# Summing two tokens' accumulators over partitions: sixteen one-column products become eight streaming products in four column groups; one bank for a pair of transposes; weight sums issued earlier

## The chip, the core and the metric

The kernel is one program on one core of a Trainium2 chip. The metric is the device time of one execution in microseconds (us); lower is better. The engines are named as in the profile: PE (TensorE matmul), PEld (its weight load), DVE (VectorE), ACT (ScalarE), POOL (GpSimd) and SP (SyncE, which here issues DMAs).

## The reference

One layer of a streaming encoder, batch 1, 1024 tokens and 16 learned meta tokens ahead of them, 1024 features:

```python
u = rmsnorm(h, norm_mix_g)
z = u @ w_in                        # q, k, v, o gates of 4 mLSTM and 4 retention heads
mixed = concat(mlstm heads, retention heads) * gates     # 2048 features
h = h + mixed @ w_out               # the mixer's output product
a = causal_dwconv(u2 @ w_up); h = h + (silu(a) * (u2 @ w_gate)) @ w_down   # u2 = rmsnorm(h)
out = rmsnorm(h, norm_final_g)[:, N_META:]
```

## The kernel before, in words

Activations lie transposed, with features on the 128 partitions and tokens in the columns; `resid` holds the residual as 8 feature blocks (KB = 8) by tokens. A matmul with full accuracy is done as three: both operands are split into a high and a low part in a rounded type, and hi*hi, lo*hi and hi*lo are added in PSUM (lines 378 to 380, 388 to 390, 554 to 556).

The program has these stages, with their times in the trace:

- **The heads**, up to about 700 us. `ORDER` is the list of heads, [4,0,1,2,3,5,6,7]; below, the place in this list is i. For each head, the o gates of this head are merged with its scan, and the v product of the next head is merged with `post_steps` of this one (norm of a head, two transposes, multiplication by the gate). `post_steps(h, p)` for the token third p returns the statistics and `half(0)`, `half(1)`. Each half takes a PSUM tile of the tag `tr`, which has one bank; transposes into it; and has DVE multiply out of it (line 908). After that, `tables(nxt)` loads the next retention head's decay table A (line 529), masks it on DVE (line 533) and scales it on ACT (line 536).
- **The output product** `mixed @ w_out`, about 700 to 863 us, by the object `mixw` in a scheme of seven products in place of eight, in steps called "1", "65", "73", "4" and "2". Its outputs are added to `resid` by DVE (lines 698 and 713). Two of the scheme's operands, called 65 and 73, are sums of blocks of w_out. They are made ahead of time in DRAM by `wsum` (lines 188 to 197): two DMAs of 512 KB on SP (line 194), then five adding DMAs on POOL (line 196), each of which waits for the one before on the same sum. There are 8 such sums "w" for w_out and 11 sums "d" for w_down. `wsum_next()` pops the next one. In the heads it is called after one of the o groups of each i from 1 to 7, and once in a v group, for i = 4.
- **The last two tokens** don't fit this scheme (columns T-2 and T-1 of `resid`). `last_two(k)` (line 178 on) loads block k of w_out and has DVE multiply it by the two tokens' values, one value per partition, and add it to the accumulator `acc` (128 partitions by 2 tokens by 1024 outputs, line 181). In the end `acc` must be summed over its partitions and added to `resid`. This is done in step "4" by lines 1186 to 1190: 16 matmuls, each with a 128x128 piece of `acc` as the stationary operand and a column of ones as the moving one, and one DVE addition of the 16 resulting columns.
- **The norm of the second half of the tokens** (514 columns, the last two among them), then the feed-forward products `pup` and `pga` from about 863 us. ACT squares each block of `resid` (line 1095), DVE adds the squares (line 1099), PE sums over partitions (`pcb`, lines 298 and 309) and spreads the result (`prb`, line 309), ACT copies it (line 313), DVE scales `resid` (line 1109), and ACT and DVE make the hi and lo operands `xh` and `xl` (lines 1037 and 1038). The quarters of the first half follow in the same manner and give `uh_g` and `ul_g`.

The order within each engine is not the order of the source: a scheduler places each instruction on its engine by estimated times, so that an edit moves its neighbours too. Pools of buffers are named by tags; `ftile` is one of five slots.

Of the kernel before, what the change touches and what calls it, by code (L numbers as in the profile page):

```python
# [17 lines left out]
P = 128  # L18
# [45 lines left out]
def body(ctx, tc, h_in, vecs, cst, mask_in, rot, w_v0, w_v, w_fm, w_out, w_up, w_gate, w_down, out):  # L64
# [133 lines left out]
    def wsum_next():  # L198
        if wsums:
            wsum(*wsums.pop(0))  # L200
# [157 lines left out]
    def v_group(h, c, tag="pp"):  # L358
        t0, L = CH[c]
        nv = 264 if h == HF else 256  # L360
        U = [need(("v", h, i), 2 - i) for i in range(2)]
        pv = pp(f"pv{h}_{c}", tag)
        if c == 0:

            for i in range(2):
                for j in range(4):
                    nc.tensor.matmul(pv[32 * j:32 * j + 32, :nv], ug[:, 4 * i + j, :], U[i][2][:, j * nv:(j + 1) * nv],
                                     start=i == 0, stop=i == 1, tile_position=(0, 32 * j))
            t = wk.tile([P, WMAX], F32, tag="cv", name=f"v0_{h}", bufs=2)[:META]
            nc.scalar.copy(t[:, :nv], pv[:META, :nv])  # L370
            for j in range(1, 4):
                nc.vector.tensor_tensor(t[:, :nv], pv[32 * j:32 * j + META, :nv], t[:, :nv], ALU.add)
            return lambda: v_evac(h, 0, META, t)
        for kb in range(KB):
            hi, lo, _ = U[kb // 4]
            o = (kb % 4) * nv
            a, b = uh[kb][:, t0:t0 + L], ul[kb][:, t0:t0 + L]
            nc.tensor.matmul(pv[:L, :nv], a, hi[:, o:o + nv], start=kb == 0, stop=False)  # L378
            nc.tensor.matmul(pv[:L, :nv], a, lo[:, o:o + nv], start=False, stop=False)  # L379
            nc.tensor.matmul(pv[:L, :nv], b, hi[:, o:o + nv], start=False, stop=kb == KB - 1)  # L380
        return lambda: v_evac(h, c, L, pv)
# [40 lines left out]
    def o_group(h, b, p):  # L422
        t0, t1, _ = PIECES[p]
        t0 = max(t0, KEEP)
        n = t1 - t0
        U = need(("o", h, b), 2)
        pt = pp(f"po{h}_{b}_{p}")
        fm_mms(pt, U, t0, t1)
        s = sig(b, p)
        nc.vector.tensor_tensor(s, pt[:, :n], Rb[:, t0:t1], ALU.mult)  # L430
        nc.scalar.activation(s, s, AF.Sigmoid if h < H else AF.Silu)
# [440 lines left out]
    def post_steps(h, p):  # L872
        t0, t1, chs = PIECES[p]
        n = len(chs)
        m = {}

        def stats():
            num, mv, base = outs.pop(p)
            z = mxp.tile([P, 4], F32, tag="z", name=f"z{h}_{p}", bufs=2)
            if h < H:  # L880
                den = base[:, 0:n, DV]
                e2 = cols[:, 2].rearrange("p (c h) -> p h c", h=H)[:, h, chs[0]:chs[0] + n]
                nc.vector.tensor_tensor(z[:, :n], den, den, ALU.mult)
                nc.vector.tensor_tensor(z[:, :n], z[:, :n], e2, ALU.max)
                nc.vector.scalar_tensor_tensor(z[:, :n], z[:, :n], EPS, mv[:, 0:n, 1], ALU.mult, ALU.add)
            else:
                nc.vector.tensor_tensor(z[:, :n], mv[:, 0:n, 1], Re[:, h - H, chs[0]:chs[0] + n], ALU.add)
            nc.scalar.activation(z[:, :n], z[:, :n], AF.Sqrt)
            nc.vector.reciprocal(z[:, :n], z[:, :n])
            nc.vector.scalar_tensor_tensor(mv[:, 0:n, 1], mv[:, 0:n, 0], -1.0, z[:, :n], ALU.mult, ALU.mult)  # L890
            for i, c in enumerate(chs):
                L = CH[c][1]
                nc.scalar.activation(num[i][:L, :DV], num[i][:L, :DV], AF.Identity, bias=mv[:L, i, 1:2], scale=z[:L, i:i + 1])
            m["num"] = num

        def half(b):
            num = m["num"]
            tr = ps.tile([P, 512], F32, tag="tr", name=f"tr{h}_{p}_{b}")
            for i, c in enumerate(chs):
                c0, L = CH[c]  # L900
                nc.tensor.transpose(tr[:, c0 - t0:c0 - t0 + L], num[i][:L, b * P:(b + 1) * P], ident[:L, :L])
            a0 = max(t0, KEEP)
            w = t1 - a0
            g = (V_MLG if h < H else V_RTG) + (h % H) * 2 + b
            i = 2 * h + b

            def mix_into(dst, x0, x1):
                nc.vector.scalar_tensor_tensor(dst, tr[:, x0 - t0:x1 - t0], vec[:, g:g + 1], sig(b, p)[:, x0 - a0:x1 - a0], ALU.mult, ALU.mult)
            if h == 7:
                for q, o in (("A2", MA), ("B2", MB)):  # L910
                    x0, x1 = max(a0, o), min(t1, o + HB)
                    if x0 < x1:
                        mix_into(wact(q, 6 + b)[:, x0 - o:x1 - o], x0, x1)
                if t1 > MB + HB:
                    mix_into(mm[:, i], MB + HB, t1)
                return
            mx = sig(b, p)
            mix_into(mx[:, :w], a0, t1)
            e = min(t1, MB + HB)
            nc.sync.dma_start(mxd[i][:, a0 - MA:e - MA], mx[:, :e - a0])  # L920
            if e < t1:
                nc.vector.tensor_copy(mm[:, i], mx[:, e - a0:w])
        return [stats, lambda: half(0), lambda: half(1)]
# [8 lines left out]
    def merge(main, side, start=0, stop=None):  # L932
        stop = len(main) if stop is None else stop
        done = 0
        for i, m in enumerate(main):
            m()
            if i + 1 > start:
                want = len(side) * min(i + 1 - start, stop - start) // (stop - start)
                while done < want:
                    side[done]()  # L940
                    done += 1
        while done < len(side):
            side[done]()
            done += 1
# [58 lines left out]
    for i, h in enumerate(ORDER):  # L1003
        A = lambda c, h=h: (lambda: scan_a(h, c))
        B = lambda c, h=h: ab(h, c)
        merge([lambda b=b, p=p: (o_group(h, b, p), p == 1 and b and i and wsum_next()) for b in range(2) for p in range(3)],
              [A(0)] + [B(c) for c in range(4 if h < 7 else NCH)])
        if h == 7:
            break
        side = post_steps(h, 0) + [B(4), B(5), B(6)] + post_steps(h, 1) + [B(7), B(8)] + post_steps(h, 2)  # L1010
        nxt = ORDER[i + 1]
        merge([lambda c=c: (v_group(nxt, c)(), c == 4 and i == 4 and wsum_next()) for c in range(NCH)], side)
        if i:
            tables(nxt)
        for kind in "qk":
            for p in range(3):
                qk_group(nxt, kind, p)
# [141 lines left out]
    for t, (st, k) in enumerate(mixw.steps):  # L1159
        if st == "2":  # L1160
            break
        if t == 0:
            mixw.pump()
        if st == "65" and k == 1:
            x = fp.tile([P, 4 * XW], F32, name="wm", tag="xh2", bufs=1)
            last_two(14, x[:, :D])
            last_two(15, x[:, D:2 * D])
        if st == "1" and k:
            mixw.tsum(1, k - 1)
        elif st == "65":  # L1170
            if k == 0:
                mixw.tsum(1, KW - 1)
            if k >= 2:
                mixw.tsum(3, k - 2)
        elif st == "73" and k < 2:
            mixw.tsum(3, KW - 2 + k)
        if t == KW - 1:
            mixw.mms(t)
        for u in range(t, min(t + (3 if st == "4" or (st, k) == ("73", KW - 1) else 2), 4 * KW)):
            mixw.prep(u)  # L1180
            if mixw.steps[u][0] == "73" and u % 2 and u + 7 not in mixw.four:
                mixw.pre4(u + 7)
        if t != KW - 1:
            mixw.mms(t)
        if st == "4" and k == 0:
            pe = pp("pe2", "tr")
            for mb in range(KB):
                for i in range(2):
                    nc.tensor.matmul(pe[:, 2 * mb + i:2 * mb + i + 1], acc[:, i, mb * P:(mb + 1) * P], cs[:, C_M01 + P - 1:C_M01 + P], start=True, stop=True)
            V.tensor_tensor(resid[:, :, T - 2:], pe[:, :2 * KB].rearrange("p (m i) -> p m i", i=2), resid[:, :, T - 2:], ALU.add)  # L1190
        if st == "4":
            some(3)
        if k == KW - 1:
            mixw.give(st)
            if st == "73":
                for b in (2, 6):
                    blocks[b] = fblock(b)
                side += norm_tasks(*BQ[0]) + scale_tasks(*BQ[0], "tr")
# [404 lines left out]
```

## Time and profile before

| | us |
|---|---|
| median of 3 runs | 1546.13 (1542.49 to 1546.73) |
| the profiled execution | 1549.12 |
| its span in the profile | 1547.3 |
| PE busy | 1524.0 (98%) |
| DVE busy | 1090.0 (70%) |
| ACT busy | 739.3 (48%) |

The profiled execution is a single one; 1.8 us of it lie outside the span. A timeline row gives start, duration, engine, line, operation and operands; what stands in brackets at its end is the idle time of the engine before it, and what ended it. "x32" on a matmul of this profile counts passes: a product of unrounded f32 operands shows two passes for each instruction.

### The profile page before, as it was taken

The numbers are of one execution on the slowest core, as the hardware profiler recorded it, in microseconds if no ns is written. First come the engines' busy times: TensorE is split into PE (matmuls) and PEld (weight loads), VectorE is DVE, ScalarE is ACT, GpSimd is POOL, SyncE is SP. The second block draws the span as 40 slices with busy tenths as digits, with TensorE's granted clock in tenths as the row PEclk, the third lists the DMA queues.
The fourth block names the chain that finished last, engine by engine and source line by source line (L and its number), as shares of the span: only waits on it lengthen the run. The fifth ranks groups of instructions, "written<-read, shape, count | busy, mean of one in ns | idle before, by whom it ended". The sixth has DMA issues, their size and how long they took to land.

```text
span 1547.3 us, 25387 instructions
## 1 busy us (share of the span) xinstructions
PE 1524.0 (98%) x9763; PEld 1400.5 (91%) x9763; DVE 1090.0 (70%) x2342; ACT 739.3 (48%) x1494; POOL 90.6 (6%) x109
## 2 busy tenths in 40 slices
PE   8999999999999999999999999999999999999997
PEld 7989999999999999997788998999999999888887
DVE  8757767676867566668867778666666666778657
ACT  7365555555543434336454555444444444434443
POOL 0001000010101000000000000211111110000000
PEclk9999999999999999999999999999999999999999
DMA  6124344262648152347542327888656567923213
GB/s 215 42 70 122 77 123 90 98 142 79 161 111 197 54 128 71 101 111 244 185 137 92 96 94 244 211 223 200 161 145 161 148 156 197 373 99 113 96 41 109
DMA packets 105192, 213.41 MB, mean 138 GB/s; under 512 B 9384, under 2 KB 31600, under 8 KB 105072
## 3 DMA queue, kind: packets, MB, share of 16 engines
q1 hardware_dynamic: 86384, 176.86, 33.6%
q0 software_dynamic: 18544, 34.87, 15.1%
q8 instruction: 76, 1.25, 0.3%
q14 instruction: 44, 0.36, 0.1%
q10 hardware_dynamic: 144, 0.07, 0.0%
HBM read 182.37 MB, written 84.19 MB: 172 GB/s over the span
## 4 chain that ended last, share of the span: by engine, by line
PE 93%; DMA 2%; DVE 2%; ACT 2%; issue 1%; SPq 0%; DVEq 0%; ACTq 0%
PE pv L378 4%; PE pv L379 4%; PE pv L380 4%; PE po L388 3%; PE po L390 3%; PE po L389 3%; PE pdx L554 3%; PE pdx L556 3%; PE pdx L555 3%; PE pup_x L555 2%; PE pup_x L556 2%; PE pga_x L554 2%; PE pga_x L556 2%; PE pga_x L555 2%; PE pup_x L554 2%; PE pwx L555 2%
## 5 line engine op out<-in xcount | busy, mean ns | idle before, releaser
L378 PE MATMUL pv<-hi_v,uh 128*128 128x256 f32 (+1 forms) x512 | 148.3, 290 | 3.1 <-ACT hi_v L151 2.1
L379 PE MATMUL pv<-lo_v,uh 128*128 128x256 f32 (+1 forms) x512 | 147.3, 288 | 0.0
L380 PE MATMUL pv<-hi_v,ul 128*128 128x256 f32 (+1 forms) x512 | 146.2, 287 | 0.0
L388 PE MATMUL po<-uh,hi_o 128*128 128x386 f32 (+2 forms) x384 | 123.9, 323 | 1.1 <-DVE kT L419 1.1
L389 PE MATMUL po<-ul,hi_o 128*128 128x386 f32 (+2 forms) x384 | 122.7, 319 | 0.0
L390 PE MATMUL po<-uh,lo_o 128*128 128x386 f32 (+2 forms) x384 | 122.6, 319 | 0.0
L378 PEld LDWEIGHTS pv<-hi_v,uh 128*128 128x128 f32 x512 | 98.2, 192 | 6.5 <-issue 2.9
L379 PEld LDWEIGHTS pv<-lo_v,uh 128*128 128x128 f32 x512 | 98.2, 192 | 0.8 <-DVE lo_v L152 0.8
L380 PEld LDWEIGHTS pv<-hi_v,ul 128*128 128x128 f32 x512 | 98.1, 192 | 0.1
L245 ACT CAST hi_up<-raw_up 128x512 fp32r<-128x512 f32 (+1 forms) x52 | 36.5, 719 | 107.7 <-PE pga_z L555 60.8
L196 POOL DMA_DIRECT2D wsd<-w_down_d x55 | 50.9, 1025 | 575.0 <-DMA wsd<-w_down_d 482.2
L196 POOL DMA_DIRECT2D wsw<-w_out_d x40 | 37.2, 1028 | 631.2 <-DMA wsw<-w_out_d 593.7
L388 PEld LDWEIGHTS po<-uh,hi_o 128*128 128x128 f32 x384 | 72.3, 188 | 1.4 <-DVE kT L419 1.2
L389 PEld LDWEIGHTS po<-ul,hi_o 128*128 128x128 f32 x384 | 72.3, 188 | 0.1
L390 PEld LDWEIGHTS po<-uh,lo_o 128*128 128x128 f32 x384 | 72.3, 188 | 0.1
L246 DVE TENSOR_TENSOR lo_ga<-fraw_ga,hi_ga 128x512 fp32r<-128x512 f32 (+1 forms) x52 | 41.9, 809 | 38.2 <-ACT hi_ga L245 37.9
L554 PE MATMUL pup_x<-uh_g,hi_up 128*128 128x256 f32 (+1 forms) x240 | 67.2, 282 | 0.4 <-ACT uh_g L1034 0.4
L555 PE MATMUL pup_x<-ul_g,hi_up 128*128 128x256 f32 (+1 forms) x240 | 67.4, 283 | 0.1
L246 DVE TENSOR_TENSOR lo_up<-raw_up,hi_up 128x512 fp32r<-128x512 f32 (+1 forms) x52 | 41.4, 810 | 35.4 <-ACT hi_up L245 34.6
L556 PE MATMUL pup_x<-uh_g,lo_up 128*128 128x256 f32 (+1 forms) x240 | 66.1, 282 | 0.0
L388 PE MATMUL pq<-uh,hi_q 128*128 128x400 f32 (+2 forms) x192 | 62.4, 325 | 0.2 <-DVE rq L409 0.2
L389 PE MATMUL pk<-ul,hi_k 128*128 128x400 f32 (+2 forms) x192 | 62.4, 325 | 0.0
(751 smaller groups left out, 5055.9 us busy)
## 6 DMA issues: line engine op xcount, KB each, us to landing
raw_up<-w_up_d SPq DMA_DIRECT2D x22, 512.0 KB, 6.6
fraw_ga<-w_gate_d SPq DMA_DIRECT2D x22, 512.0 KB, 3.8
acts<-cv SPq DMA_DIRECT2D x44, 256.0 KB, 5.8
wsd<-w_down_d SPq DMA_DIRECT2D x22, 512.0 KB, 7.8
wsd<-w_down_d POOLq DMA_DIRECT2D x22, 512.0 KB, 6.6
rd<-wsd SPq DMA_DIRECT2D x22, 512.0 KB, 3.5
wsd<-w_down_d POOLq DMA_DIRECT2D x33, 256.0 KB, 7.2
raw_o<-w_fm_d SPq DMA_DIRECT2D x16, 512.0 KB, 3.6
```

What stands on the lines that cost most here:

```text
L196: nc.gpsimd.dma_start(x, v, accum_op=ALU.add)
L245: nc.scalar.copy(hi[:, o:o + n], x)
L246: nc.vector.tensor_tensor(lo[:, o:o + n], x, hi[:, o:o + n].bitcast(F32), ALU.subtract)
L378: nc.tensor.matmul(pv[:L, :nv], a, hi[:, o:o + nv], start=kb == 0, stop=False)
L379: nc.tensor.matmul(pv[:L, :nv], a, lo[:, o:o + nv], start=False, stop=False)
L380: nc.tensor.matmul(pv[:L, :nv], b, hi[:, o:o + nv], start=False, stop=kb == KB - 1)
L388: nc.tensor.matmul(pt[:, :n], a, uh[kb][:, t0:t1], start=kb == 0, stop=False)
L389: nc.tensor.matmul(pt[:, :n], a, ul[kb][:, t0:t1], start=False, stop=False)
L390: nc.tensor.matmul(pt[:, :n], b, uh[kb][:, t0:t1], start=False, stop=kb == KB - 1)
L554: m.append(nc.tensor.matmul(pt, ah, xh_, start=first and k == 0, stop=False, skip_group_check=True))
L555: nc.tensor.matmul(pt, ah, xl_, start=False, stop=False, skip_group_check=True)
L556: m.append(nc.tensor.matmul(pt, al, xh_, start=False, stop=last and k == n - 1, skip_group_check=True))
```

## The change

Three edits.

1. In `half(b)`, for the last third (p == 2), both halves use one bank: the second half's transposes go to columns behind the first's, rather than into a new tile of the same tag.
2. The o groups call `wsum_next()` for 0 < i < 6 only, and the v groups for i = 3, 4 and 5. So the eight sums are made by i = 5 instead of i = 7.
3. The sum over partitions turns round. `pick` is a small stationary operand, 128x32, zero but for a column of ones. `acc` streams: for each of the two tokens, four matmuls of 256 columns go to four column groups of PE (32 output partitions each). ACT copies the 128x256 result back, into `acc`; after the products of that step, two 128x128 transposes bring it to features on partitions, and two DVE additions, each of 128x4x2 elements, replace the one addition.

```diff
-            tr = ps.tile([P, 512], F32, tag="tr", name=f"tr{h}_{p}_{b}")
+            if b == 0 or p < 2:
+                m["tr"] = ps.tile([P, 512], F32, tag="tr", name=f"tr{h}_{p}_{b}")
+            tr = m["tr"][:, b * (t1 - t0):] if p == 2 else m["tr"]
...
-        merge([lambda b=b, p=p: (o_group(h, b, p), p == 1 and b and i and wsum_next()) for b in range(2) for p in range(3)],
+        merge([lambda b=b, p=p: (o_group(h, b, p), p == 1 and b and 0 < i < 6 and wsum_next()) for b in range(2) for p in range(3)],
...
-        merge([lambda c=c: (v_group(nxt, c)(), c == 4 and i == 4 and wsum_next()) for c in range(NCH)], side)
+        merge([lambda c=c: (v_group(nxt, c)(), c == 4 and 2 < i < 6 and wsum_next()) for c in range(NCH)], side)
...
+        if st == "4" and k == 0:
+            pe, n = pp("pe2", "tr"), D // 4
+            pick = ftile("pick")[:, :64].rearrange("p (t j) -> p t j", t=2)
+            nc.gpsimd.memset(pick, 0.0)
+            for i in range(2):
+                nc.gpsimd.memset(pick[:, i, i:i + 1], 1.0)
+            for i in range(2):
+                for j in range(4):
+                    nc.tensor.matmul(pe[32 * j:32 * j + 32, :n], pick[:, i, :], acc[:, i, j * n:(j + 1) * n], start=i == 0, stop=i == 1, tile_position=(0, 32 * j))
+            nc.scalar.copy(acc[:, 0, :n], pe[:, :n])
         if t != KW - 1:
             mixw.mms(t)
         if st == "4" and k == 0:
-            pe = pp("pe2", "tr")
-            for mb in range(KB):
-                for i in range(2):
-                    nc.tensor.matmul(pe[:, 2 * mb + i:2 * mb + i + 1], acc[:, i, mb * P:(mb + 1) * P], cs[:, C_M01 + P - 1:C_M01 + P], start=True, stop=True)
-            V.tensor_tensor(resid[:, :, T - 2:], pe[:, :2 * KB].rearrange("p (m i) -> p m i", i=2), resid[:, :, T - 2:], ALU.add)
+            for i in range(2):
+                nc.tensor.transpose(pe[:, n + i * P:n + (i + 1) * P], acc[:, 0, i * P:(i + 1) * P], ident)
+                x = resid[:, i:KB:2, T - 2:]
+                V.tensor_tensor(x, pe[:, n + i * P:n + (i + 1) * P].rearrange("p (j t) -> p j t", t=32)[:, :, 0:2], x, ALU.add)
```

How the instructions lie on the engines, before and now. On PE in step "4" of the output product, before (`pwx` are the product's accumulators, `pe` the two tokens' sums):

```order
L554 MATMUL pwx_8884<-rr_8821,w4xh_9352 128x512
L555 MATMUL pwx_8884<-rr_8821,w4xh_9352 128x512
L556 MATMUL pwx_8884<-rr_8821,w4xl_9353 128x512
L554 MATMUL pwx_8888<-rr_8821,w4xh_9352 128x512
L1189 MATMUL pe_9661<-cs,acc 128x1 x16
L555 MATMUL pwx_8888<-rr_8821,w4xh_9352 128x512
```

At the same place on PE now:

```order
L554 MATMUL pwx_8876<-rr_8813,w4xh_9344 128x512
L555 MATMUL pwx_8876<-rr_8813,w4xh_9344 128x512
L556 MATMUL pwx_8876<-rr_8813,w4xl_9345 128x512
L554 MATMUL pwx_8880<-rr_8813,w4xh_9344 128x512
L1193 MATMUL pe_9641<-acc,pick 32x256 x8
L555 MATMUL pwx_8880<-rr_8813,w4xh_9344 128x512
```

The sums stand at the same place of the stream. The two transposes (line 1199) follow 22 and 47 rows later, each alone among 512-column products.

On PE further on, around the spreading product `prb` of the second half's norm, before (`pwy` are the scheme's last products):

```order
L556 MATMUL pwy_9872<-wr_00_9856,wl_9921 128x256
L554 MATMUL pwy_9864<-wr_10_9861,wl_9920 128x256
L309 MATMUL prb_9749<-cs,rcolb_9738 128x128 x4
L555 MATMUL pwy_9864<-wr_10_9861,wl_9920 128x256
L556 MATMUL pwy_9864<-wr_10_9861,wl_9921 128x256
```

And the same product now:

```order
L556 MATMUL pwy_9860<-wl_9872,wl_9913 128x256
L554 MATMUL pwy_9864<-wl_9872,wl_9844 128x256
L309 MATMUL prb_9741<-cs,rcolb_9730 128x128 x4
L555 MATMUL pwy_9864<-wl_9873,wl_9844 128x256
L556 MATMUL pwy_9864<-wl_9872,wl_9845 128x256
```

It has moved 76 rows down PE's list (from row 5348 to row 5424), and the first product that reads `xl` from row 5426 to row 5475; 78 rows lay between the two before, 51 lie between them now. In the next norm, that of the first half's last quarter, `prb` moves from row 5618 to row 5654.

On SP around the fourth of the sums, before (`raw_v`, `raw_q`, `raw_k`, `raw_o` are loads of weights, `mxd` stores, A the decay table):

```order
L148 DMA raw_q_0_4463<-w_fm_d 128x1024
L148 DMA raw_k_0_4953<-w_fm_d 128x1024
L148 DMA raw_o_0_4959<-w_fm_d 128x1024
L920 DMA mxd_98<-sig 128x386
L920 DMA mxd_99<-sig 128x386
L529 DMA A_190<-scr 128x8x128
L529 DMA A_189<-scr 128x8x128
L920 DMA mxd_98<-sig 128x384
L148 DMA raw_o_1_5067<-w_fm_d 128x1024
L194 DMA wsw_3_132<-w_out_d 256x1x512
```

And now:

```order
L148 DMA raw_q_0_4460<-w_fm_d 128x1024
L194 DMA wsw_3_132<-w_out_d 256x1x512
L194 DMA wsw_3_140<-w_out_d 256x1x512
L148 DMA raw_k_0_4956<-w_fm_d 128x1024
L148 DMA raw_o_0_4962<-w_fm_d 128x1024
L922 DMA mxd_98<-sig 128x386
L922 DMA mxd_99<-sig 128x386
L529 DMA A_190<-scr 128x8x128
```

The sum has moved ahead of the loads of `raw_k`, `raw_o` and of the table A of that head.

## The prediction

> **What bounds the kernel now.** I read the page first, for the engine that sets the end: the busy shares and the chain that ended last.
>
> ```profile
> PE 1524.0 (98%) x9763; PEld 1400.5 (91%) x9763; DVE 1090.0 (70%) x2342; ACT 739.3 (48%) x1494; POOL 90.6 (6%) x109
> PE 93%; DMA 2%; DVE 2%; ACT 2%; issue 1%; SPq 0%; DVEq 0%; ACTq 0%
> ```
>
> PE has next to no gaps. An edit therefore counts by what it takes out of PE's stream, and by the waits that it makes or ends there. Next, PE's timeline around the sixteen one-column products:
>
> ```profile
> 828.46 0.39 PE L554 MATMUL pwx<-rr,w4xh 128*128 128x512 f32 x1
> 828.69 4.54 PE L1189 MATMUL pe<-cs,acc 128*128 128x1 f32 x32
> 833.09 0.77 PE L555 MATMUL pwx<-rr,w4xh 128*128 128x512 f32 x1
> ...
> 838.21 0.39 PE L555 MATMUL pwx<-rr,w4xh 128*128 128x512 f32 x1
> ```
>
> The sums hold PE from 828.69 to 833.09, 4.40 us. Ahead of them a 512-column product takes 0.23 us to the next start (828.46 to 828.69); behind them 12 starts, from 833.09 to 838.21, take 5.12 us, 0.43 each. The windows give the reason, by the column PEclk (the second last but two):
>
> ```profile
> 831.00:832.00 1.00, 1.00 (x7) 1.00 (x8) 0.00 (x0) 0.00 (x0) 0.00 (x0) 0.59 0.00 0
> 833.00:838.00 5.00, 5.00 (x14) 3.94 (x14) 3.20 (x6) 4.52 (x9) 0.00 (x0) 0.50 0.75 281
> ```
>
> In the sums, between 831 and 832, the granted clock falls, and it is 0.50 to 838, although PE is counted as busy without a break.
>
> **The sum over partitions: what goes.** The block itself, 4.40 us, and what the low clock costs the products behind it: the 12 starts in 5.12 us would take 2.76 at 0.23, so 2.36 are lost. Together 6.76 us.
>
> **What comes in its place.** The same form (a 128x32 stationary, 256 columns, four column groups, eight instructions of two passes) is in the v groups already, line 367:
>
> ```profile
> 185.75 0.28 PE L823 MATMUL n<-S_2h,qd_3h 128*128 128x258 f32 x1
> 185.96 0.63 PE L367 MATMUL pv<-raw_v,ug 128*32 128x256 f32 x4
> 186.52 0.39 PE L824 MATMUL n<-S_2l,qd_3h 128*128 128x258 f32 x1
> 186.74 0.28 PE L825 MATMUL n<-S_2h,qd_3l 128*128 128x258 f32 x1
> 186.95 1.06 PE L367 MATMUL pv<-raw_v,ug 128*32 128x256 f32 x12
> 187.94 0.39 PE L378 MATMUL pv<-hi_v,uh 128*128 128x256 f32 x1
> 188.16 0.28 PE L379 MATMUL pv<-lo_v,uh 128*128 128x256 f32 x1
> 185.00:189.00 4.00, 4.00 (x36) 2.72 (x35) 3.25 (x13) 2.66 (x8) 0.00 (x0) 1.00 0.11 29
> ```
>
> From 186.74 to 188.16 lie twelve passes and two ordinary products of 0.12 each (the spacing of such products; 78 rows take 10 us further below): 1.42 - 0.24 = 1.18 us. From 185.75 to 186.74 lie four passes and two such products: 0.75. So eight more passes cost 0.43, and sixteen in a row about 1.40. The bounds are 1.18, if the last four are free, and 16 x 0.12 = 1.9, if the groups gain nothing; I take 1.4, since line 367 is the same instruction. [...]
>
> The clock stays at 1.00 around line 367, so I charge no half clock.
>
> The two transposes, of the shape of line 901:
>
> ```profile
> 658.30 0.34 PE L389 MATMUL pk<-ul,hi_k 128*128 128x384 f32 x1
> 658.47 0.34 PE L390 MATMUL pk<-uh,lo_k 128*128 128x384 f32 x1
> 658.65 0.38 PE L901 MATMUL tr<-cs,num 128*128 128x128 f32 x2
> ...
> 659.05 0.34 PE L389 MATMUL pk<-ul,hi_k 128*128 128x384 f32 x1
> ```
>
> From 658.47 to 659.05 two of them and two products of 0.17 (658.30 to 658.47) take 0.58, so the pair costs 0.24; apart, each with its own edge, at most twice that. I take 0.3. The ACT copy and the two DVE additions are hidden on PE: 22 rows of 0.23 us lie between the sums and the first transpose, far more than a copy. PE's own account is thus -6.76 + 1.40 + 0.30 = -5.06 us. The memsets of `pick` are POOL's, which is 6% busy: nothing.
>
> **What the new place of the norm costs.** The second half's norm can't start before the second transpose, 47 rows behind the sums (10.9 us at 0.23, so near 841.2, where the squares start now at 833.5). Its stages slide down PE's list against the products that read their results. What covers them now:
>
> ```profile
> PE pup_x L554 <- ACT uh_g L1034: 0.4, 1, 0.4
> 856.96 1.05 PE L309 MATMUL prb<-cs,rcolb 128*128 128x128 f32 x8
> 863.85 0.75 DVE L1038 SCALAR_TENSOR_TENSOR xl<-resid,vec,xh 128x514 fp32r<-128x514 f32 x1
> 866.97 0.28 PE L555 MATMUL pup<-xl,hi_up 128*128 128x256 f32 x1
> 893.47 0.61 PE L309 MATMUL prb<-cs,rcolb 128*128 128x128 f32 x4
> 897.26 1.67 DVE L1038 SCALAR_TENSOR_TENSOR ul_g<-resid,vec,uh_g 128x258 fp32r<-128x258 f32 x4
> 899.83 0.28 PE L555 MATMUL pup<-ul_g,hi_up 128*128 128x258 f32 x1
> ```
>
> The first row is all that PE waits from 820 to 960. From `prb` at 856.96 to the first `xl` (863.85 + 0.75) it takes 7.64 us, and PE reads it 10.01 us after `prb`, 78 rows on (0.118 a row beside some 0.8 for `prb` itself). Now 51 rows lie between: 27 fewer are 3.19 us, so PE comes at 6.82, and waits 0.8 us. In the next norm, from `prb` at 893.47 to the first `ul_g` (a quarter of 1.67 behind 897.26) are 4.21 us, and PE reads it after 6.36; the 35 rows that `prb` loses to it are 4.13 us, so PE would come at 2.2 and wait 2.0. Bounds: nothing, if DVE and ACT, with other work ahead of these stages gone by then, run them faster than now; 5.6 us, if both waits double. I take 0.8 + 2.0 = 2.8.
>
> **The weight sums.** One of them is issued on SP at the end of the heads (i = 7) now, just ahead of the last two loads of `raw_m`. The second of these is waited for:
>
> ```profile
> 656.57 0.87 SPq L178 DMA_DIRECT2D raw_m<-w_out_d  x1
> 666.84 2.48 DVE L181 SCALAR_TENSOR_TENSOR acc<-raw_m,mm,acc 128x1024 f32<-128x1024 f32 x2 [4.63 <-DMA raw_m<-w_out_d]
> 671.10 0.44 PE L388 MATMUL po<-uh,hi_o 128*128 128x384 f32 x1 [1.06 <-DVE kT L419]
> DMA to landing us min/median/max: 3.6/7.2/10.2
> ```
>
> It took 10.2 us, from its issue at 656.57, the longest of its kind (last row); DVE waited 4.63 us for it, and `kT`, queued behind, kept PE 1.06 us. At the median of 7.2 us the load would come 3.0 earlier, and PE's wait is gone: -1.06 (bound 0, if the load is slow for another reason). The sum at i = 6 goes too; PE has no wait there: 0. Two sums come, at i = 3 and 5. For i = 3 the load that matters is the table A:
>
> ```profile
> 386.92 1.23 DVE L533 TENSOR_TENSOR A<-A,mask 128x1024 f32<-128x1024 f32 x1 [2.16 <-DMA A<-scr]
> 395.22 0.48 ACT L353 ACTIVATE vh<-pv,Rc 128x256 fp32r<-128x256 f32 x1 [2.43 <-PE n L825]
> DMA to landing us min/median/max: 4.7/4.7/4.7
> ```
>
> A lands 4.7 us after its issue and DVE already waits for it, but ACT waits 2.43 us for PE afterwards. A delay of up to 2.4 us is covered, and costs nothing; the bound above is the slow rival below. On SP the sum's two issues now stand ahead of `raw_k`, `raw_o` and A; two times the 0.87 us of an issue are within that cover too, and POOL has nothing else behind its adding DMAs. At i = 5 no table is loaded: 0.
>
> **The shared bank** spares the second transposes of a pair the wait for the first half's multiplication. PE waits at such a place only for the last head:
>
> ```profile
> 740.03 0.41 PE L901 MATMUL tr<-cs,A 128*128 128x128 f32 x2 [0.79 <-DVE mm L908]
> 741.23 0.47 PE L554 MATMUL pwy<-wtq,hi_w 128*128 128x512 f32 x1 [0.80 <-DVE mm L908]
> ```
>
> The first wait goes, but the second is for DVE's work in its own order, and comes out as much longer: 0 (at best -0.1).
>
> **The sum:** -5.06 + 2.8 - 1.06 = -3.3 us. The profiled execution, 1549.12, becomes 1545.8; against the median of the runs shown, 1546.13, about 3.0 below it, it is 1542.8. A measurement of this kernel can tell some 0.3%, 4.6 us, from no change.
>
> **The rivals.** (1) *The whole gain comes through.* The two waits of 2.8 us don't arise, because ACT and DVE have idle time and run the norm's stages as soon as their inputs are there. Then -5.06 - 1.06 = -6.1: 1540.0 by the median. For it: DVE's own waits ahead of these stages; against it: the rows of PE's list, which fix when `prb` comes. Over 4.6 us needs 1.3 us less wait than I count. (2) *The clock falls nevertheless.* Sixteen passes with a 32-column stationary are still poor work for PE, as the one-column ones were; against it stands 1.00 around line 367. A half-clock stretch of 3.4 us costs 1.7, two of them 3.4: -1.6 to +0.1, 1544.5 to 1546.2. [...] (3) *The norm is late by more*: both waits double: -3.3 + 2.8 = -0.5, 1545.6. (4) *Slower.* The five adding DMAs of the sum moved to i = 3 are still under way when A is loaded, and those at i = 5 slow the loads of the weights that stand behind them on SP. If such a load takes 10.2 us, as `raw_m` did, instead of 4.7, it is 5.5 late, 2.43 are covered, and PE waits 3.1; a wait of two us brings half clock:
>
> ```profile
> 100.12 0.39 PE L823 MATMUL u<-vh,kwh 128*128 128x256 f32 x1 [1.97 <-DVE C L861]
> 101.00:104.00 3.00, 3.00 (x16) 3.00 (x15) 2.85 (x8) 3.00 (x10) 0.00 (x0) 0.50 0.00 1
> ```
>
> Three us at 0.50 are 1.5 more, 4.6 for each place, 9.2 for both: +5.9, 1552.0. It decides from a landing of 7.1 us on; against it, the sum at i = 4 in the kernel before has the same company and leaves no wait on PE.
>
> **How the numbers follow.** The forecast (waits of 1.5 to 4.5 us in the norms) 0.43; (1) 0.38; (2) 0.07; (3) 0.06; (4) 0.06. Faster by over 0.3% is (1), 0.38; slower is (4), 0.06; the rest, 0.56, is within. The range goes from (1) with the shortest block and no edge at the transposes, -6.5, and a median's scatter of 1 us, 1538.6, up to (3) with the longest block and without the 1.06: +1.1, so 1547.2. That leaves out (4) and some of (2).
>
> **What would show it.** Right: a block of line 1193 of 1.2 to 1.9 us; clock 1.00 from 828 to 840; the second addition near 841; PE waits for `xl` near 868 and `ul_g` near 895, 2 to 3 us in all; no wait for `kT` near 671. Wrong: half clock behind the block; no waits in the norms (then 1540); PE waits between 360 and 400 or 525 and 560 of over 1 us.

## The result, and the profile after

| | before | after |
|---|---|---|
| median, us | 1546.13 (1542.49 to 1548.14, 5 runs) | 1554.29 (1552.91 to 1556.48, 5 runs) |
| ratio to before | | 1.0057, 95% interval 1.0042 to 1.0073 |
| span of the profiled execution, us | 1547.3 | 1551.7 |

The changed kernel is slower by 0.57%, some 8.8 us (6.5 to 11.3). The forecast was 1542.8, within 1538.6 to 1547.2: wrong in sign and outside its range. The two profiled executions differ by 4.4 us only; that of before was 1549.12, 3 us above its median, so the traces show about half of the difference, and single waits in them have to be tested by repetition.

The page of the changed kernel, the lines that answer to those of before:

```profile
span 1551.7 us, 25373 instructions
PE 1522.4 (98%) x9749; PEld 1396.6 (90%) x9749; DVE 1089.4 (70%) x2343; ACT 739.1 (48%) x1495; POOL 91.1 (6%) x112
PE 85%; DVE 5%; ACT 4%; DMA 4%; issue 1%; SPq 0%; DVEq 0%; ACTq 0%
```

PE is busy 1.6 us less, as an edit that takes work from it should make it. But the chain that ended last runs through DVE, ACT and DMA for 13% where it was 6%, and PE stands idle for 29.3 us of the span (the span less its busy time) where it was 23.3.

The block itself, on PE's timeline of the changed kernel:

```profile
832.02 0.40 PE L554 MATMUL pwx<-rr,w4xh 128*128 128x512 f32 x1
832.35 1.07 PE L1193 MATMUL pe<-acc,pick 128*32 128x256 f32 x16
833.35 0.50 PE L555 MATMUL pwx<-rr,w4xh 128*128 128x512 f32 x1
...
838.34 0.27 PE L1199 MATMUL pe<-cs,acc 128*128 128x128 f32 x1
...
844.01 0.27 PE L1199 MATMUL pe<-cs,acc 128*128 128x128 f32 x1
```

Sixteen passes now hold PE for 1.2 us (from 832.25, where the next product was due, to 833.35, and 0.11 at the edge behind), the transposes for 0.1 each, and the windows show full clock right through:

```profile
828.00:838.00 10.00, 10.00 (x56) 7.44 (x55) 4.04 (x7) 5.21 (x13) 0.00 (x0) 1.00 0.00 0
901.00:905.00 4.00, 4.00 (x22) 4.00 (x23) 3.96 (x11) 1.28 (x5) 0.00 (x0) 0.60 0.00 0
```

The low clock has come back at another place, 901 to 905 (second row). The waits of PE from 820 to 960, one row of 0.4 us before, are four:

```profile
PE pup L555 <- DVE ul_g L1040: 1.7, 1, 1.7
PE pup_x L554 <- ACT uh_g L1036: 1.2, 1, 1.2
PE pga L554 <- ACT hi_ga L245: 0.8, 1, 0.8
PE pup L555 <- DVE xl L1040: 0.4, 1, 0.4
```

The waits for `xl` and `ul_g` are the norm's, as forecast; those for `hi_ga` and for more of `uh_g` the forecast did not have. The rows of the second half's norm and of the last quarter's:

```profile
864.19 1.05 PE L309 MATMUL prb<-cs,rcolb 128*128 128x128 f32 x8
870.74 0.75 DVE L1040 SCALAR_TENSOR_TENSOR xl<-resid,vec,xh 128x514 fp32r<-128x514 f32 x1
871.55 0.39 PE L555 MATMUL pup<-xl,hi_up 128*128 128x256 f32 x1 [0.39 <-DVE xl L1040]
...
896.66 0.61 PE L309 MATMUL prb<-cs,rcolb 128*128 128x128 f32 x4
900.39 1.68 DVE L1040 SCALAR_TENSOR_TENSOR ul_g<-resid,vec,uh_g 128x258 fp32r<-128x258 f32 x4
900.93 0.39 PE L555 MATMUL pup<-ul_g,hi_up 128*128 128x258 f32 x1 [1.70 <-DVE ul_g L1040]
```

In the heads there is a loss where the forecast put nothing. At the start of the head after i = 3, before:

```profile
410.92 0.33 SPq L148 DMA_DIRECT2D raw_v<-w_v_d  x1
417.12 1.05 ACT L151 CAST hi_v<-raw_v 128x1024 fp32r<-128x1024 f32 x1 [9.37 <-DMA raw_v<-w_v_d]
425.60 0.34 PE L823 MATMUL u<-vh,kwh 128*128 128x258 f32 x1
```

And after, with the wait for the table A ahead of it:

```profile
389.16 1.23 DVE L533 TENSOR_TENSOR A<-A,mask 128x1024 f32<-128x1024 f32 x1 [3.79 <-DMA A<-scr]
413.04 0.33 SPq L148 DMA_DIRECT2D raw_v<-w_v_d  x1
421.73 1.05 ACT L151 CAST hi_v<-raw_v 128x1024 fp32r<-128x1024 f32 x1 [11.75 <-DMA raw_v<-w_v_d]
430.14 0.39 PE L823 MATMUL u<-vh,kwh 128*128 128x258 f32 x1 [2.49 <-ACT kwh L806]
430.00:434.00 4.00, 3.86 (x15) 3.75 (x16) 3.72 (x11) 2.56 (x8) 0.00 (x0) 0.59 0.00 0
```

The load of `raw_v` takes 8.69 us from its issue to ACT's reading, where it took 6.20; `kwh` stands behind that on ACT (8.0 us after it in both traces), PE waits 2.49 us for it, and half clock follows (0.59 in the window). From the first row of line 367 of one head to that of the next, 356.8 to 441.0 before, it is 357.4 to 447.1 now: 5.5 us more.

### The profile page after: what moved, and what is told of

Same layout as the page of the kernel before. It is cut to its first block, busy times and chain, and to the rows that moved or that the text cites. A ratio compares the mean times of both kernels' runs of the same rounds, so it can differ in the third digit from the quotient of the medians.

```text
span 1551.7 us, 25373 instructions
## 1 busy us (share of the span) xinstructions
PE 1522.4 (98%) x9749; PEld 1396.6 (90%) x9749; DVE 1089.4 (70%) x2343; ACT 739.1 (48%) x1495; POOL 91.1 (6%) x112
## 4 chain that ended last, share of the span: by engine, by line
PE 85%; DVE 5%; ACT 4%; DMA 4%; issue 1%; SPq 0%; DVEq 0%; ACTq 0%
PE pv L378 3%; PE pv L379 3%; PE pv L380 3%; PE po L390 3%; PE po L388 3%; PE po L389 3%; PE pdx L554 3%; PE pdx L556 3%; PE pdx L555 3%; PE pup_x L555 2%; PE pup_x L556 2%; PE pga_x L554 2%; PE pga_x L556 2%; PE pga_x L555 2%; PE pup_x L554 2%; PE pdy L554 2%
```

## The experiments

Each was timed in 5 rounds beside the kernel before; where nothing else is said, the edit is made to the kernel before. Lines of a trace are of one profiled execution.

**The three edits apart** (e1 to e4). e1 is the first hunk of the diff alone, e2 the two `wsum_next` hunks, e3 the last hunk, and e4 the changed kernel with this put back:

```diff
-... p == 1 and b and 0 < i < 6 and wsum_next()     # o group
+... p == 1 and b and i and wsum_next()
-... c == 4 and 2 < i < 6 and wsum_next()           # v group
+... c == 4 and i == 4 and wsum_next()
```

> Only the shared bank. The theory (the loss lies in the heads, where loads of raw_v come late beside the weight sums' adding DMAs, and in the feed-forward's start, where the norm is late): the bank's edit does nothing, the time is that of the kernel before within 2 us. Rival, the bank itself delays the heads (transposes of the second half wait for the first's bank, DVE is held): 3 to 8 us slower, with PE waits in the heads at 253, 340 and 421 us as in the changed kernel.

> Only the weight sums moved earlier. The theory: the wait of 1.06 us at 671 goes, but the first load of raw_v between 410 and 422 lands 8 us or more after its issue instead of 6.2, PE waits for kwh and the clock halves: 2 to 6 us slower than before. Rival, the late raw_v is chance and the sums' place does not matter: 1 us faster to no difference, and raw_v's landings scatter as in the kernel before.

> Only the sum over partitions with the ones held. The theory: some 5.5 us are gained at the block and about as much is lost at the feed-forward's start (waits for xl, ul_g, hi_ga and uh_g and one stretch of half clock): within 2 us of the kernel before. Rival, this edit carries the whole loss: 4 to 8 us slower. Second rival, the forecast's own: 2 to 3 us faster.

> The changed kernel with the weight sums put back (bank and sum over partitions stay). The theory: the loss of the sums' move, 2 to 6 us, is undone, and the time is within 2 us of the kernel before, 1546 to 1549. Rival, the sums are harmless: 1552 to 1556 as the changed kernel.

| | ratio to before | interval | in us |
|---|---|---|---|
| e1, bank | 0.9999 | 0.9986 to 1.0012 | 0 |
| e2, weight sums | 1.0033 | 1.0017 to 1.0048 | +5.1 |
| e3, sum over partitions | 1.0026 | 1.0011 to 1.0041 | +4.0 |
| e4, bank and sum over partitions | 1.0027 | 1.0016 to 1.0038 | +4.2 |

The bank changes nothing that can be told from the scatter. The two other edits lose about equally and add up: 0.33 + 0.26 = 0.59%, against 0.57% for the whole. My theory at that point had the sums right (though `raw_v` took 7.57 us in e2, not 8 or more), but e3 and e4 wrong: I had expected them within 2 us of before, and they are 4 us slower. A reason is in the trace of e1, which has the old sixteen products:

```profile
823.40 3.63 PE L1191 MATMUL pe<-cs,acc 128*128 128x1 f32 x32
826.89 0.48 PE L555 MATMUL pwx<-rr,w4xh 128*128 128x512 f32 x1
...
823.00:830.00 7.00, 7.00 (x48) 6.34 (x47) 2.86 (x5) 3.52 (x8) 0.00 (x0) 1.00 0.28 104
```

Here the same sixteen products take 3.49 us and no half clock comes with them or after them. So half of what the block seemed to cost is not always there (counted further down).

**Where the sum over partitions loses: e7.** Both transposes first, then one DVE addition; otherwise as e3:

```diff
             for i in range(2):
                 nc.tensor.transpose(pe[:, n + i * P:n + (i + 1) * P], acc[:, 0, i * P:(i + 1) * P], ident)
-                x = resid[:, i:KB:2, T - 2:]
-                V.tensor_tensor(x, pe[:, n + i * P:...].rearrange("p (j t) -> p j t", t=32)[:, :, 0:2], x, ALU.add)
+            x = resid[:, :, T - 2:].rearrange("p (j i) t -> p j i t", i=2)
+            V.tensor_tensor(x, pe[:, n:n + 2 * P].rearrange("p (i j t) -> p j i t", i=2, t=32)[:, :, :, 0:2], x, ALU.add)
```

> Only the sum over partitions, but with the two transposes side by side and one DVE addition behind both. The theory (the loss is the norm's, whose start hangs on the second transpose, which the first addition holds back by 25 rows): PE's waits for xl near 866 and ul_g near 895 go, and the time is 1.5 to 4 us below the kernel before. Rival, the streaming products or the ACT copy themselves cost: as the run with the bare sum over partitions, 3 to 5 us slower than before.

Ratio 0.9985 (0.9972 to 0.9998), 2.3 us faster than before and some 6 us faster than e3, with the same products, copy and transposes. On PE the second transpose has moved up beside the first, so `prb` of the second half moves up by 50 rows, and that of the last quarter lies 44 rows ahead of the first product that reads `ul_g` instead of 16. The trace:

```profile
832.96 0.38 PE L1197 MATMUL pe<-cs,acc 128*128 128x128 f32 x2
859.65 0.75 DVE L1038 SCALAR_TENSOR_TENSOR xl<-resid,vec,xh 128x514 fp32r<-128x514 f32 x1
865.18 0.28 PE L555 MATMUL pup<-xl,hi_up 128*128 128x256 f32 x1
...
PE pup_x L554 <- ACT uh_g L1034: 1.2, 1, 1.2
```

`xl` is ready at 860.4 and read at 865.18, nearly 5 us later; from 820 to 960 only the wait for `uh_g` is left. The loss of e3 was thus the norm's late start, and the late start came of the addition between the two transposes: in e3 the scheduler put the second transpose behind the first addition, 25 rows down PE's list. Both touch the same PSUM tile, which may be why; no run gave them two tiles. The wait for `uh_g` is as long here as in e3 (1.2 us, 0.4 before), so that part is not the late start's.

**Which of the moved sums loses: e6 and e8.** e6 moves only the sum of i = 7 (to the v group of i = 5); e8 adds one at i = 3 and none at i = 5:

```diff
-... p == 1 and b and i and wsum_next()
+... p == 1 and b and 0 < i < 7 and wsum_next()
-... c == 4 and i == 4 and wsum_next()
+... c == 4 and 3 < i < 6 and wsum_next()           # e6
+... c == 4 and 2 < i < 5 and wsum_next()           # e8
```

> The sums moved for i = 7 only: its sum goes to the v group of i = 5, nothing is added at i = 3. The theory (the loss comes from the sum at i = 3, beside the table A): no loss, the time of the kernel before, 0 to 2 us faster; no PE wait between 380 and 430. Rival, any sum added in a v group costs its share: 2 to 3 us slower.

> One sum is added in the v group of i = 3, none at i = 5; the sum of i = 7 is gone from there. The theory: the whole loss of the moved sums stands, 3 to 6 us slower than before, with a DVE wait of 3.5 us or more for A near 386 and a PE wait of 2 us or more near 426. Rival, the two added sums share the loss: 1 to 2.5 us slower.

e6: 0.9996 (0.9986 to 1.0007), nothing lost. e8: 1.0021 (1.0006 to 1.0035), +3.2 us, and in its trace DVE waits 3.80 us for A and PE 2.25 us near 429. The loss is that of the sum at i = 3.

**How it loses: e5, e9, e12, e13, e14, e15.** The two symptoms were a late A and, 30 us on, a late `raw_v`. e9 makes A late without a sum:

```diff
+            if h == 3 and x == 0:
+                nc.sync.dma_start(a[:, META + 4 * P:].rearrange("p (c t) -> p c t", t=P), src[x, h, 5:].partition_broadcast(P))
             nc.sync.dma_start(a[:, META:].rearrange("p (c t) -> p c t", t=P), src[x, h, 1:].partition_broadcast(P))
```

> The kernel before, with the second half of table A loaded twice for the head after i = 3, so that the full load starts only when the first has landed; no weight sum moves. DVE gets A 2 to 4 us later, as beside the sum at i = 3. The theory that A's lateness is the way of the loss: raw_v near 410 is issued and lands later too, PE waits 2 us or more for kwh near 426, 2 to 5 us slower. Rival, the added sum's traffic or its position among the sums does it: a wait of at most 1 to 2 us near 390 and none near 426, 0 to 2 us slower.

```profile
387.13 0.61 DVE L910 SCALAR_TENSOR_TENSOR sig<-tr,vec,sig 128x384 f32<-128x384 f32 x1
391.62 1.23 DVE L535 TENSOR_TENSOR A<-A,mask 128x1024 f32<-128x1024 f32 x1 [3.87 <-DMA A<-scr]
413.39 0.33 SPq L148 DMA_DIRECT2D raw_v<-w_v_d  x1
418.89 1.05 ACT L151 CAST hi_v<-raw_v 128x1024 fp32r<-128x1024 f32 x1 [3.00 <-DMA raw_v<-w_v_d]
426.92 0.39 PE L825 MATMUL u<-vh,kwh 128*128 128x258 f32 x1 [0.53 <-ACT kwh L808]
```

Ratio 1.0001 (0.9987 to 1.0015). A is worked on 4.7 us later than before, more than in the changed kernel, and `raw_v` is issued 2.5 us later, but it lands in 5.50 us, PE waits 0.53, and nothing is lost. So a late A does not make `raw_v` slow. Whether a late A costs something by itself e9 does not test: the edit moved a multiplication by the gate, `sig`, ahead of A on DVE (first row), and in the kernels with the moved sum it stands behind A, with PE waiting for it. In e2:

```profile
386.53 1.23 DVE L533 TENSOR_TENSOR A<-A,mask 128x1024 f32<-128x1024 f32 x1 [4.75 <-DMA A<-scr]
388.07 0.61 DVE L908 SCALAR_TENSOR_TENSOR sig<-tr,vec,sig 128x384 f32<-128x384 f32 x1
388.73 0.44 PE L901 MATMUL tr<-cs,num 128*128 128x128 f32 x2 [1.17 <-DVE sig L908]
```

DVE waits for A 1.63, 1.64, 2.59 and 3.90 us longer than before in the changed kernel, e8, e2 and e15, and PE then waits 0.22, 0.22, 1.17 and 2.48 us for `sig`: 1.4 us are covered each time, the rest is PE's. The late A and the slow `raw_v` are two losses beside each other.

e5 exchanges the fourth and fifth sum, e14 does so with two tiny DMAs at i = 3, e13 has these alone, e15 is e8 with the two sums exchanged, and e12 is e8 with the moved sum's five adding DMAs left out (that sum, and what is computed from it, is incomplete there):

```diff
+    wsums[3], wsums[4] = wsums[4], wsums[3]                                   # e5, e14, e15
...
+        if (g, k) == ("w", 3):                                                # e12, ahead of the adding DMAs
+            return
...
+    def two_more():                                                           # e13, e14: called in the v group, c == 4 and i == 3
+        for j in range(2):
+            after(nc.sync.dma_start(spare[j:j + 1], w_out[j, 0:1]), last["raw"])
```

> The kernel before, with the fourth and the fifth weight sum made in the other order; no sum moves in time. Theory of the blocks: the sum of the fifth block is slower beside the load of raw_v near 410 us, wherever it comes from in the program; then raw_v lands 7.5 to 8.7 us after its issue instead of 6.0 to 6.4, PE waits some 2.3 us for kwh near 425, with half clock behind, and the time is 2 to 4 us longer. Rival, the place decides (the table A's delay at 386 pushes the later loads): no wait there, raw_v in 6.0 to 6.4, the time of the kernel before within 1.5 us.

> As the run with one sum moved to i = 3, but that sum is left incomplete: its two copies on SP stay, its five adding DMAs on POOL are left out. Theory of the adding DMAs: without them A lands as in the kernel before (DVE waits 2.2 us for it), and raw_v near 411 lands within 6.7 us; no PE wait over 1 us near 426, the time of the kernel before or 1 us below. Rival, the two more DMAs on SP (or the fifth block's sum at i = 4) do it: raw_v takes 7.5 us or more and PE waits 2 us near 426.

> The kernel before, with two tiny DMAs (4 KB each) on SP in the v group of i = 3, at the place of the moved sum's copies; no sum moves. Theory of the adding DMAs: nothing changes, raw_v near 411 lands in 5.7 to 6.7 us. [...]

> The kernel before with the fourth and fifth sum in the other order and the two tiny DMAs on SP in the v group of i = 3. Theory of a meeting of the two (the fifth block's sum at i = 4, and SP's later DMAs shifted by two): raw_v near 411 takes 7.5 us or more, PE waits 2 us near 426, 2 to 4 us slower. Rival, neither is the cause, the moved sum's own copies are: raw_v in 5.7 to 6.7 us, no loss.

> One sum moved to i = 3, as in the earlier run, but it is the fifth block's, and the fourth block's stays at i = 4. Theory that the block added at i = 4 matters: raw_v near 411 lands in 6.0 to 6.7 us as in the kernel before, no PE wait near 426, within 1.5 us of the kernel before (A is late still). Rival, a sum at i = 3 is enough whatever its block: raw_v takes 7.5 us or more, PE waits 2 us or more, 2 to 5 us slower.

| | a sum's copies at i = 3 | `raw_v`, issue to reading, us | PE's wait for `kwh`, us | ratio (interval) |
|---|---|---|---|---|
| e5 | no | 5.68 | 0 | 1.0002 (0.9990 to 1.0014) |
| e13 | no, two tiny DMAs | 6.08 | 0 | 0.9984 (0.9970 to 0.9997) |
| e14 | no, two tiny DMAs | 6.84 | 0.35 | 0.9993 (0.9982 to 1.0004) |
| e12 | yes, without the adds | 8.45 | 2.47 | 1.0008 (0.9997 to 1.0019) |
| e15 | yes | 7.88 | 2.46 | 1.0015 (1.0005 to 1.0026) |
| e8 | yes | 7.60 | 2.25 | 1.0021 (1.0006 to 1.0035) |
| e2 | yes | 7.57 | 2.25 | 1.0033 (1.0017 to 1.0048) |

The rows of e12, where no adding DMA ran at i = 3 (its trace, and that of e13 behind it):

```profile
411.56 0.33 SPq L148 DMA_DIRECT2D raw_v<-w_v_d  x1
420.01 1.05 ACT L151 CAST hi_v<-raw_v 128x1024 fp32r<-128x1024 f32 x1 [11.50 <-DMA raw_v<-w_v_d]
428.43 0.58 PE L825 MATMUL u<-vh,kwh 128*128 128x258 f32 x1 [2.47 <-ACT kwh L808]
...
DMA packets 827, 1.85 MB, mean 185 GB/s; under 512 B 69, under 2 KB 232, under 8 KB 825
```

```profile
411.44 0.33 SPq L148 DMA_DIRECT2D raw_v<-w_v_d  x1
417.52 1.05 ACT L151 CAST hi_v<-raw_v 128x1024 fp32r<-128x1024 f32 x1 [9.13 <-DMA raw_v<-w_v_d]
...
DMA packets 994, 2.10 MB, mean 210 GB/s; under 512 B 96, under 2 KB 352, under 8 KB 992
```

All five traces with the moved sum's copies (the last four of the table and the changed kernel) have `raw_v` at 7.6 to 8.7 us and a PE wait of over 2 us; all traces without them have 5.5 to 6.8. So what makes `raw_v` slow is not the block that is summed at i = 4 (e5, e14, e15), not two more places in SP's list (e13), and not the moved sum's adding DMAs (e12): each of these theories of mine fell. Why two copies of 512 KB, issued some 50 us earlier, slow a later load is not settled. What the traces show is that the DMA engines mostly move less in the 10 us from 4 us ahead of the issue (last row of each fence, 1.85 MB against 2.10; the changed kernel, e2 and e8 1.92 to 1.94, but e15 2.04 and e14, without the copies, 2.03). The load is not alone in being slow: the adding DMA of 512 KB that is issued beside it lands in 7.5 to 8.8 us in the five, and in 6.4 to 7.3 in before, e5, e6, e13 and e14, though the sum at i = 4 is made in the same way in all.

The measured time follows these waits only in part. From the first row of line 367 of this head to that of the next it takes 87.1 to 91.2 us in the five traces and 84.1 to 85.2 in the twelve others. But e12 and e15, with 88.6 and 91.2 in their traces, were timed at +1.2 us (-0.5 to +2.9) and +2.3 us (0.8 to 4.0): for e12 the slow load is shown, and a loss of time is not. And e13, which adds nothing but two tiny DMAs, measures 2.5 us faster than before, so that single differences of some 2.5 us, those of e7 and e15 from before too, are at the edge of what these runs can tell; e3 and e7, 6 us apart, are far beyond it.

**Versions that could beat both: e10 and e11.** e10 is e7 with the shared bank and e6's places. e11 is e7 with no sum in the o group of i = 3:

```diff
-... p == 1 and b and i and wsum_next()
+... p == 1 and b and i in (1, 2, 4, 5, 6) and wsum_next()
-... c == 4 and i == 4 and wsum_next()
+... c == 4 and 3 < i < 7 and wsum_next()
```

> The shared bank, the sum over partitions with the two transposes side by side, and the weight sums moved for i = 7 only (to the v group of i = 5). The theory: none of the three losses is left, and the gains of the parts stand: 1 to 4 us below the kernel before. Rival, the parts' gains are within the scatter: no difference.

> The sum over partitions with the transposes side by side, and no weight sum in the o group of i = 3: from there on each is made one call later, in the o groups of i = 4, 5, 6 and the v groups of i = 4, 5, 6. The theory that a sum's adding DMAs beside the first load of raw_v are what makes PE wait for kwh: the wait of 1.4 to 2.5 us near 340 goes, 2 to 5 us below the kernel before. Rival: the wait stays, as it has another cause, or a new one comes at i = 6: as the run with the side-by-side transposes.

e10: 0.9989 (0.9975 to 1.0003), not to be told from before or from e7. e11: 0.9962 (0.9946 to 0.9977), median 1540.74, 5.9 us faster than before. In e7, the head at 325 has a `raw_v` of 7.7 us beside that sum, and a wait:

```profile
325.40 0.33 SPq L148 DMA_DIRECT2D raw_v<-w_v_d  x1
333.08 1.05 ACT L151 CAST hi_v<-raw_v 128x1024 fp32r<-128x1024 f32 x1 [10.73 <-DMA raw_v<-w_v_d]
341.50 0.39 PE L823 MATMUL u<-vh,kwh 128*128 128x258 f32 x1 [1.85 <-ACT kwh L806]
```

In e11 no sum is made there, the load takes 3.7 us, and the wait is gone:

```profile
322.69 0.33 SPq L148 DMA_DIRECT2D raw_v<-w_v_d  x1
326.42 1.05 ACT L151 CAST hi_v<-raw_v 128x1024 fp32r<-128x1024 f32 x1 [6.79 <-DMA raw_v<-w_v_d]
337.12 0.28 PE L823 MATMUL u<-vh,kwh 128*128 128x258 f32 x1
```

In all sixteen other traces a sum is made beside this load, with no copies some 50 us ahead, and the load takes 7.05 to 9.13 us.

## Why the prediction was wrong, point by point

- **The sums: the failed step with the most weight.** The forecast gave the sum at i = 3 a price of 0 (covered) and the one that leaves i = 7 a gain of 1.06; edit 2 measures +5.1 us (e2). The gain was chance in the one trace shown: in the eight other traces that keep a sum at i = 7 (e1, e3, e4, e5, e7, e9, e13, e14), the wait for `kT` near 671 is 0 six times, and 0.29 and 0.38. The loss is of the kind of rival (4), at one of its two places (at i = 5 an added sum costs nothing that can be measured, e6). The step that failed first is "a delay of up to 2.4 us is covered": the cover was read from ACT's wait for PE, but PE waits for DVE's `sig` behind A, where only 1.4 us are covered. A was waited for 3.8 to 6.1 us (e2, e8, e15, after) instead of 2.2, and PE waited 0.2 to 2.5. Then comes `raw_v` at the next head, which the forecast didn't look at. I asked what the accumulating DMAs meet in the stage where they are put, and not what the head after it finds. With a wait of 2.25 us, half clock behind it (1.7) and 1.17 at A, the trace of e2 gives 5.1. That it meets the measured 5.1 is partly luck: the same terms in the trace of e15 (2.46, 1.7, 2.48) give 6.6, and 2.3 was measured. Rival (4) had 0.06.
- **The block's price was a sample at the upper end.** From the product ahead of the sums to the fifteenth row behind them, before took 10.21 us, and the changed kernel 4.70. But in the ten other kernels with the old block the same stretch took 10.22 once, 8.60 to 8.63 five times, and 7.05 or 7.06 four times; with the new block it was 4.69 or 4.70 in all six. So the removal brings 5.5, 3.9 or 2.4 us, 3.6 in the mean, not the 5.36 of -6.76 + 1.40. The new block's own price was right (1.2 for 1.4), and so were the transposes (0.2 for 0.3).
- **The norm: mechanism right, size short.** Forecast: 0.8 for `xl` and 2.0 for `ul_g`. Measured: 0.39 and 1.70. From `prb` to `ul_g` it takes 4.15 us (4.21 forecast), and to the reader without its wait 2.57 (2.2 forecast). What was missing: 0.8 for `hi_ga` and 0.8 more for `uh_g` behind them, and half clock after the waits. (The 0.8 for `uh_g` is in e7, e10 and e11 too, where the norm is not late; what makes it stays open.) I priced half clock behind a wait in rival (4), and left it out here: it was 1.7 us in the traces of after and e4, and 3.4 in that of e3. Waits of 3.7 and half clock of 2.3 in the mean make 6.0, so that edit 3 comes to -3.6 + 0.2 + 6.0 = +2.6, within the measured 1.7 to 6.3; the forecast had -2.3.
- **The shared bank** was right at 0 (e1), but not by the way that was forecast: the first of the two waits does not go and the second does not grow. They are 0.70 and 0.79 us in e1, where they were 0.79 and 0.80.
- **Rival (2)**, the clock falling at the new block, did not happen: 1.00 from 828 to 838. The 3.4 us of a stretch in its price are what the traces show: in before, half clock lasts 3.4 us from 100.7 to 104.1 and 6.8 from 831.2 to 838.0, and in the changed kernel 3.4 from 901.8 to 905.2 (0.50 in each whole us between). In these traces the clock fell behind waits of 1.70 (901), 2.49 (430) and even 1.21 us (934, in e4). It stayed at 1.00 behind waits of 1.78 (99) and 1.20 us (943) in the changed kernel and of 1.83 us (340) in before, and did not fall behind 1.85 (341, in e7) and 2.47 us (341, in e9) either: for such waits the measurement decides, the price is 0 or 1.7 us, and the wait's length alone does not tell which.

Together, +5.1 (measured) and +2.6 (added up) to +4.0 (measured) are 7.7 to 9.1 us, and 8.8 was measured.

## What to carry to other kernels

Where one engine is busy for 98%, a saving on it counts only if the work that hangs on the moved result keeps its lead: count the rows between the producing step and its reader in both orders, and beside each wait that arises reckon with half clock behind it, which cost 0 or 1.7 us here. A cost that is read from one profiled execution and hangs on the granted clock or on a DMA's landing is a sample; look for the same place in other traces before taking it as removed. Background DMAs are best put where no engine waits for a load, also in the stage that follows: taking one sum away from beside a load brought some 3.6 us (e11 against e7, which were not timed beside each other), and the whole rewrite of the sum over partitions 2.3 (e7). The two intervals are too wide to say which is more.

## What the runs showed of the hardware

The same sixteen one-column products cost PE three different times in eleven kernels (10.2, 8.6 and 7.05 us for the same stretch), in steps of 1.6 us: with two stretches of half clock of some 3.4 us, one, or none (3.41, 1.7 or 0 us lost by the granted clock; two are the 0.50 from 831.2 to 838.0 in before, none is the 1.00 from 823 to 830 in e1). What decides between them was not shown: no run moved the block by a known time. And in five of five traces a load took 7.6 to 8.7 us, where it took 5.5 to 6.8 in the twelve others, behind two copies that had been issued some 50 us before it. That stays without an explanation.
